# Moving the sample group's state steps beside other projection pairs, and four more gates into pairs, in a one-layer hybrid decoder step

## The chip, the cores and the metric

The kernel runs on one core of one Trainium2 chip, in one launch, and computes one trunk layer in float32. The metric is the time of one execution on the device in microseconds (us). Before the change the median of three runs is 2546.53 us (2541.39 to 2547.61).

## The reference

A prompt group (1024 tokens) and a sample group (8 sequences of one token) go through the same layer. One combined projection `w_in` feeds a gated short convolution, a Mamba-2 state-space branch (SSD) and a cross-attention; sigmoid gates weigh the three outputs.

```python
sc_b, sc_c, sc_x, z, xbc, dt_raw, q, gates = split(xn @ w_in)           # columns 1024,1024,1024,2048,3072,32,1024,3072
y_a = (sc_b * conv3(sc_c * sc_x)) @ w_sc_out
xs, bm, cm = split(silu(conv4(xbc) + b))                                # 32 heads x 64; 4 groups of B and C rows, state 128
dt = softplus(dt_raw + bias);  a = -exp(a_log)
prompt: chunked scan over 8 chunks of 128 tokens, per group of 8 heads
sample: s = s * exp(dt*a) + (dt*x) outer B;   y = s . C                 # one step on a given state, per sequence and head
y_b = group_rmsnorm((y + d*xs) * silu(z)) @ w_ssm_out
y_c = attention(q, mem_k, mem_v) @ w_attn_o
merged = sigmoid(g_a)*y_a + sigmoid(g_b)*y_b + sigmoid(g_c)*y_c;  x += merged @ w_merge_o;  x += swiglu(rmsnorm(x))
```

The sample group's state is 8 sequences x 32 heads x 64 x 128 floats. It is read from HBM, updated once and written back.

## The kernel before, in words

The 1032 tokens (1024 and 8) lie along the free dimension, the features on 128 partitions. A matmul of full precision is three passes over split operands (a high half, made by a cast on ACT, and a low half, made by a subtraction on DVE). A plain projection of 128 columns is `gemm`: 8 slices of k, three passes, three column pieces of 344, so 72 matmuls. Two such projections can be done together by `strassen` as a **pair**: seven half-size products of 24 matmuls of 258 columns, so 168 matmuls. Names of pairs are letter and column block: X (xBC), Z, G (gates), C and B (short convolution). So G0 does gates 0 and 1.

Inside a pair the products run in this order: A (into the accumulator `pa`), T1 (into `pb`), nT2 (into `pa` again, after ACT has copied A's result out, line 299), B21 (into `pc`), T3 (onto `pa`, after ACT's copy of line 321), B22 (onto `pb`), T4 (onto `pa`, after DVE's line 334 has read what T3 left there). Line 227 casts the high halves of the weight forms A, S, T, D on ACT, line 228 makes their low halves on DVE. In instruction names `X4Ah` is the high half of form A of pair X4, `X4Tl` the low half of form T.

The projections come in stages. First z, B and C rows; then 32 pairs from X17 to G14; then the SSD scan of four groups, whose pieces (`ssd_pieces`, `z_pieces`, `group_norm`) are called between the slices of plain projections ("fillers": 8 of q, 8 of gates 16 to 23, then the 8 of `w_sc_out`) by `tick`, at 6.5 pieces a projection; then attention, the other output projections, the merge and the feed-forward part.

In the stage of pairs, blocks i = 0 to 3 are X(4i), X(4i+2), then `sc_pairs(2i)` (pairs C, C, B with their convolutions), then G(4i), G(4i+2). The sample group's steps of group i (`s_pieces`: 8 states) are put into the queue `pend` ahead of `sc_pairs` and are taken three to a pair, where `strassen` calls `tick`. One state is a tile of 128 x 512 in one of two buffers (`act_tile`, tags "ah" and "al", of each of which one buffer is free in this stage): SP loads it from HBM together with its B and C rows, ACT scales its four quarters (line 811), DVE adds (line 813) and reduces (line 817), SP stores it back. The next state in the same buffer can be loaded when the store has landed.

The order of code gives precedence only. The framework that builds the program orders each engine's instructions itself, from the dependences; an instruction may stand well ahead of its place in the code, and on the chip each engine and each DMA queue (SP's, ACT's) runs its list strictly in order.

Of the kernel before, what the change touches and what calls it, by code (L numbers as in the profile page):

```python
# [41 lines left out]
def tile_kernel(ctx: ExitStack, tc, a, o):  # L42
# [611 lines left out]
    def sc_pairs(ct):  # L654
# [22 lines left out]
        o = []  # L677

# [122 lines left out]
    def s_load(g, b):  # L801
        t = act_tile(("ah", "al")[b % 2], f"st{g}_{b}", F32)
        SY.dma_start(b3(t[:, :512], 4), s_rows(a["state_ssm"], g, b))
        SY.dma_start(b3(t[:, 512:768], 2), bc_d[g, b].unsqueeze(0).to_broadcast([P, 2, P]))
        samp[g, b] = t

    def s_step(g, b):
        t = samp[g, b]
        st, junk = b3(t[:, :512], 4), t[:, 768:896]
        for i in range(4):  # L810
            S.activation(st[:, i], st[:, i], AF.Copy, scale=es[:, g * 4 + i, b : b + 1])  # L811
        for i in range(4):
            V.scalar_tensor_tensor(  # L813
                st[:, i], t[:, 512:640], dts[:, g * 4 + i, b : b + 1], st[:, i], op0=ALU.mult, op1=ALU.add
            )
        for i in range(4):
            V.scalar_tensor_tensor(  # L817
                junk, st[:, i], 1.0, t[:, 640:768], op0=ALU.mult, op1=ALU.mult,
                accum_out=ys[:, g * 4 + i, b : b + 1],
            )  # L820

    def s_store(g, b):
        SY.dma_start(s_rows(o["s_ssm"], g, b), b3(samp.pop((g, b))[:, :512], 4))

    def s_pieces(g):

        out = [lambda: s_load(g, 0)]
        for b in range(0, NS, 2):
            out.append(lambda b=b: (s_step(g, b), s_load(g, b + 1)))
            out.append(lambda b=b: (s_store(g, b), s_step(g, b + 1)))  # L830
            out.append(lambda b=b: (s_store(g, b + 1), s_load(g, b + 2) if b + 2 < NS else None))
        return out

    def ssd_pieces(g, xg, bcg):
# [131 lines left out]
        out = [head]  # L966
# [100 lines left out]
    pend.extend([dt_softplus, dt_sums, dt_rows, dt_sample])  # L1067
# [73 lines left out]
    def mem_rms():  # L1141
# [3 lines left out]
        rsqrt(pm, mrs, mst, D, [P, 2], "m")  # L1145

    def mem_t(m, half):
        if half == 0:
            V.tensor_scalar(mem_sb[m], mem_sb[m], mrs[:, m : m + 1], None, op0=ALU.mult)
# [62 lines left out]
    bc_rows()  # L1212
    for i in range(4):
# [11 lines left out]
    pend.extend([None, lambda: b12s.extend(again(rb))])  # L1225
    z_pair(14)
# [639 lines left out]
```

## Time and profile before

| | |
|---|---|
| three runs | 2541.39, 2547.61, 2546.53 us; median 2546.53 |
| profiled execution | 2541.26 us, of which 2539.5 us between the first and the last instruction (the span) |
| busy | PE 2468.5 us, DVE 1512.5, ACT 1029.7, POOL 130.0 |
| stage of pairs, X17 to G14 | 279.67 to 945 us of the span |
| SSD with its fillers | 945 to 1360 us |
| attention and output projections, merge, feed-forward | 1360 to the end |
| DMA | 394.72 MB, mean 155 GB/s |

PE is TensorE, DVE VectorE, ACT ScalarE, POOL GpSimd; SP issues DMAs. A row of the chain or the timeline begins with its start and its length in us. `out<-in` names what is written and read, `xN` the count. `[1.3 <-DMA st]` is the idle time before the instruction and what ended it. Busy PE is not PE at its peak, since matmuls overlap; idle PE is what the tables of waits list.

### The profile page before, as it was taken

What the parts mean: (1) busy time and instruction counts of PE and PEld (TensorE: products, weight loads), DVE (VectorE), ACT (ScalarE), POOL (GpSimd) and SP (SyncE); (2) the same over time, 40 slices, a digit from 0 to 9 for tenths busy, and PEclk for the clock granted to TensorE, in tenths of its full rate; (3) what the DMA queues carried; (4) which work ended last, traced back from release to release, by engine and by line L of the source; (5) the groups of instructions that cost most, each with busy time, mean ns of one, the idle gap of its engine ahead of it and who ended that gap; (6) DMA issues with size and microseconds to landing.
All of it is one profiled execution on the core that took longest, in us unless ns stands there. A gap on an engine that the chain in (4) does not pass through costs nothing.

```text
span 2539.5 us, 44748 instructions
## 1 busy us (share of the span) xinstructions
PE 2468.5 (97%) x18594; PEld 2400.7 (95%) x18594; DVE 1512.5 (60%) x2570; ACT 1029.7 (41%) x1664; POOL 130.0 (5%) x163
## 2 busy tenths in 40 slices
PE   7999999999999999999999989999999999999998
PEld 5999999999999998999989888999999999999998
DVE  6753588486776845665777672444776444453316
ACT  6554454354444445455544341213443333341202
POOL 0300000000000002121120000000000000000000
PEclk9999999999999999999999999999999999999999
DMA  6244435243342555755778977844442222274211
GB/s 203 88 150 158 126 105 155 96 147 119 111 147 80 174 182 168 234 178 188 260 222 281 305 260 239 301 145 151 143 145 93 84 68 84 75 237 139 75 34 68
DMA packets 351610, 394.72 MB, mean 155 GB/s; under 512 B 15798, under 2 KB 289318, under 8 KB 351399
## 3 DMA queue, kind: packets, MB, share of 16 engines
q1 hardware_dynamic: 332254, 338.90, 42.5%
q10 hardware_dynamic: 19153, 52.96, 5.5%
q8 instruction: 146, 2.39, 0.4%
q14 instruction: 57, 0.47, 0.1%
HBM read 283.57 MB, written 108.45 MB: 154 GB/s over the span
## 4 chain that ended last, share of the span: by engine, by line
PE 79%; DVE 9%; DMA 7%; ACT 2%; issue 2%; SPq 0%; POOL 0%; ACTq 0%; DVEq 0%
PE po L195 11%; PE pd L195 8%; PE pm L1624 4%; PE ps_g L195 3%; PE ps_q L195 3%; PE py L906 1%; PE pss L924 1%; PE po L898 1%; DVE ax L649 1%; PE ps_z L195 1%; DMA st<-bc_d 1%; PE X17m L240 1%; PE u20m L240 1%; PE G14m L240 1%; PE G12m L240 1%
## 5 line engine op out<-in xcount | busy, mean ns | idle before, releaser
L1766 DVE TENSOR_TENSOR x<-pd,x 128x1032 f32<-128x1032 f32 x24 | 29.6, 1231 | 127.9 <-PE pd L195 127.9
L853 ACT ACTIVATE r<-r,acum 128x128 f32<-128x128 f32 x256 | 78.7, 391 | 6.0 <-DMA r<-ac_d 5.4
L1265 DVE TENSOR_TENSOR gt<-po,gt 128x1032 f32<-128x1032 f32 x24 | 29.5, 1231 | 58.1 <-PE po L195 54.6
L811 ACT ACTIVATE st<-st,es 128x128 f32<-128x128 f32 x128 | 42.3, 395 | 50.7 <-DMA st<-in_state_ssm_dram 43.7
L885 POOL TENSOR_TENSOR xdd<-xdt,decst 128x512 f32<-128x512 f32 x32 | 40.7, 1271 | 316.6 <-DVE xdt L881 316.6
L649 DVE SCALAR_TENSOR_TENSOR ax<-u,prm,ax 128x1024 f32<-128x1024 f32 x44 | 56.4, 1282 | 0.0
L813 DVE SCALAR_TENSOR_TENSOR st<-st,dts 128x128 f32<-128x128 f32 x128 | 41.6, 348 | 18.8 <-ACT st L811 9.4
L879 DVE TENSOR_TENSOR r<-r,cbm 128x1024 f32<-128x1024 f32 x32 | 39.1, 1221 | 9.8 <-ACT r L854 8.5
L878 ACT COPY bT<-bp 128x128 f32<-128x128 f32 x32 | 8.4, 264 | 88.6 <-DVE cbm L876 88.5
L906 PE MATMUL py<-r,xdt 128*64 128x128 f32 x512 | 35.8, 283 | 4.9 <-issue 4.9
L915 DVE SCALAR_TENSOR_TENSOR x<-x,dpar,yt 128x128 f32<-128x128 f32 x128 | 36.4, 347 | 4.6 <-ACT yt L913 3.8
L817 DVE SCALAR_TENSOR_TENSOR st<-st 128x128 f32<-128x128 f32 x128 | 36.7, 287 | 0.8
L906 PEld LDWEIGHTS py<-r,xdt 128*64 128x64 f32 x512 | 27.9, 139 | 9.2 <-issue 5.8
L902 DVE TENSOR_TENSOR yt<-po,ea 128x512 f32<-128x512 f32 x28 | 19.4, 691 | 28.0 <-PE po L898 28.0
L924 PE MATMUL pss<-xdd,bT 128*128 128x512 f32 x64 | 33.0, 598 | 1.1 <-ACT bT L878 1.0
L854 ACT ACTIVATE r<-r 128x1024 f32<-128x1024 f32 x32 | 33.8, 1058 | 0.5
L937 POOL TENSOR_TENSOR s<-s,cdec 128x512 f32<-128x512 f32 x28 | 33.0, 1178 | 18.9 <-DVE s L930 17.3
L1553 DVE TENSOR_TENSOR gt<-po,gt 128x1032 f32<-128x1032 f32 x8 | 9.9, 1232 | 39.3 <-PE po L195 39.3
L1631 DVE TENSOR_TENSOR x<-pm,xT 128x516 f32<-128x516 f32 x16 | 11.1, 696 | 36.2 <-PE pm L1624 36.1
L1374 DVE SCALAR_TENSOR_TENSOR kc<-kc,qb 128x256 f32<-128x256 f32 x64 | 23.9, 420 | 13.5 <-DMA qb<-qs_d 9.1
L898 PE MATMUL po<-bc,s 128*128 128x128 f32 x224 | 30.1, 278 | 0.0
L898 PEld LDWEIGHTS po<-bc,s 128*128 128x128 f32 x224 | 28.1, 191 | 0.7
(8997 smaller groups left out, 8863.4 us busy)
## 6 DMA issues: line engine op xcount, KB each, us to landing
gt<-gt_d SPq DMA_DIRECT2D x32, 516.0 KB
r<-ac_d SPq DMA_DIRECT2D x32, 512.0 KB
mg_d<-gt SPq DMA_DIRECT2D x24, 516.0 KB
mg<-mg_d SPq DMA_DIRECT2D x24, 516.0 KB
xs_d<-ax ACTq DMA_DIRECT2D x22, 516.0 KB
hr<-h_d SPq DMA_DIRECT2D x22, 516.0 KB
gt_d<-G ACTq DMA_DIRECT2D x16, 516.0 KB
x<-xs_d SPq DMA_DIRECT2D x16, 516.0 KB
```

The costliest lines, as they stand in the source:

```text
L195: PE.matmul(ps[:, n, :CW], wt[:, ks], x[:, n * CW : (n + 1) * CW], start=(k == 0 and i == 0), stop=(k == nk - 1 and i == 2),)
L240: PE.matmul(ps[:, n, :HC], wt[:, ks], x[:, n * HC : (n + 1) * HC], start=(start and kt == 0 and i == 0), stop=(kt == 3 and i == 2), skip_g ...
L649: V.scalar_tensor_tensor(acc[:, :T], u[:, j : j + T], w[j], acc[:, :T], op0=ALU.mult, op1=ALU.add)
L811: S.activation(st[:, i], st[:, i], AF.Copy, scale=es[:, g * 4 + i, b : b + 1])
L813: V.scalar_tensor_tensor(st[:, i], t[:, 512:640], dts[:, g * 4 + i, b : b + 1], st[:, i], op0=ALU.mult, op1=ALU.add)
L853: S.activation(r[:, j, :], r[:, j, :], AF.Relu, scale=-1.0, bias=acum[:, c, h : h + 1])
L879: V.tensor_tensor(r, r, bc(cbm.unsqueeze(1), [P, HPG, P]), op=ALU.mult)
L885: G.tensor_tensor(b3(xdd, HPG), b3(xdt, HPG), bc(decst[:, c, hs].unsqueeze(2), [P, HPG, 64]), op=ALU.mult)
L898: PE.matmul(po[:, t * P : (t + 1) * P], state["s"][:, t * P : (t + 1) * P], bcg[1][:, cs], start=True, stop=True,)
L906: PE.matmul(py[hp : hp + 64, (h // 2) * P : (h // 2 + 1) * P], xdt[:, h * 64 : (h + 1) * 64], r[:, (h % 2) * 4 + h // 2, :], start=True, s ...
L924: PE.matmul(pss, bT, xdd, start=True, stop=True)
L1624: PE.matmul(ps[:, n, :HC], wt[:, ks], x[:, half * HT + n * HC : half * HT + (n + 1) * HC], start=(k == 0 and i == 0), stop=(k == KD - 1 an ...
```

## The change

Six edits:

1. The order of a block becomes X(4i), G(4i), X(4i+2), G(4i+2), C, C, B.
2. The sample group's steps become a list of 34 slots (`s_slots`): slot n stores the previous tile if n is even, does state n, and after an odd n loads the next tile. A tile holds two states (128 x 1024), the B and C rows of four states come in one load of their own (`sr`). Slots are taken three to each pair G and to Z14, two to each pair B and to G16; none in the code of X and C pairs (and none in G0).
3. Gates 16 to 19 become pairs G16 and G18; the fillers of the SSD are now 12 and 8 (q, gates 20 to 23, `w_sc_out`), and the pace is the count of pieces over 20, which is 7.9.
4. The loads of the first SSD group move from the first filler into G18 (`plain`, after T3), and the first weights of q with them; four empty slots follow the group's head.
5. The step sizes (`dt_softplus` and what follows) come one tick later.
6. The scaling of both halves of the memory (`mem_rms`) comes one tick earlier.

```diff
@@ sc_pairs, before the pair B
+        pend.extend([steps.popleft() for _ in range(2)])
@@
-    def s_load(g, b):
-        t = act_tile(("ah", "al")[b % 2], f"st{g}_{b}", F32)
-        SY.dma_start(b3(t[:, :512], 4), s_rows(a["state_ssm"], g, b))
-        SY.dma_start(b3(t[:, 512:768], 2), bc_d[g, b].unsqueeze(0).to_broadcast([P, 2, P]))
-        samp[g, b] = t
+    def s_load(p):
+        g, b = divmod(2 * p, NS)
+        if p % 2 == 0:
+            samp["r"] = ev_tile(f"sr{p}")
+            rows_ = bc_d[g, b : b + 4].rearrange("b w p -> (b w p)")
+            SY.dma_start(samp["r"][:, :1024], rows_.unsqueeze(0).to_broadcast([P, 1024]))
+        samp[p] = act_tile(("ah", "al")[p % 2], f"st{p}", F32), samp["r"]
+        for i in range(2):
+            SY.dma_start(b3(samp[p][0][:, 512 * i : 512 * i + 512], 4), s_rows(a["state_ssm"], g, b + i))
...
-    def s_pieces(g):
-        out = [lambda: s_load(g, 0)]
-        for b in range(0, NS, 2):
-            out.append(lambda b=b: (s_step(g, b), s_load(g, b + 1)))
-            out.append(lambda b=b: (s_store(g, b), s_step(g, b + 1)))
-            out.append(lambda b=b: (s_store(g, b + 1), s_load(g, b + 2) if b + 2 < NS else None))
-        return out
+    def s_slots():
+        n_all = GROUPS * NS
+        steps.append(lambda: s_load(0))
+        for n in range(n_all + 1):
+            def slot(n=n):
+                if n % 2 == 0 and n > 0:
+                    s_store(n // 2 - 1)
+                if n < n_all:
+                    s_step(n)
+                if n % 2 == 1 and n + 1 < n_all:
+                    s_load((n + 1) // 2)
+            steps.append(slot)
+
+    def with_steps(n, pair):
+        pend.extend([steps.popleft() for _ in range(n)])
+        pair()
@@ ssd_pieces
-        out = [head]
+        out = [head] + ([None] * 4 if g == 0 else [])
@@
-    pend.extend([dt_softplus, dt_sums, dt_rows, dt_sample])
+    pend.extend([None, dt_softplus, dt_sums, dt_rows, dt_sample])
@@ mem_rms (from mem_t)
+        for m in range(2):
+            V.tensor_scalar(mem_sb[m], mem_sb[m], mrs[:, m : m + 1], None, op0=ALU.mult)
@@
     for i in range(4):
         xbc_pair(4 * i, 4 * i + 1)
+        with_steps(3 if i else 0, lambda: gate_pair(4 * i))
         xbc_pair(4 * i + 2, 4 * i + 3)
-        pend.extend(s_pieces(i))
+        with_steps(3, lambda: gate_pair(4 * i + 2))
         sc_pairs(2 * i)
-        gate_pair(4 * i)
-        if i < 3:
-            gate_pair(4 * i + 2)
-    flush()
+    with_steps(3, lambda: z_pair(14))
+    with_steps(2, lambda: gate_pair(16))
...
     def plain():
+        loaded["wq0"] = load_raw(wblock(w_in, C_Q), "wq0")
+        load_group(0)
         for kt in range(4):
             split_to(*xforms["T3"][kt], b12s[kt // 2][:, HS[kt % 2]])
-    gate_pair(14, plain)
+    gate_pair(18, plain)
...
-    for i in range(16, 24):
+    for i in range(20, 24):
         fillers.extend(gate_step(i))
...
-    pace[0] = 6.5
-    while pend:
+    pace[0] = len(pend) / (len(fillers) + KD)
+    while fillers or pend:
```

What the engines' lists become at three places. In the names below `st_6107` is the fifth tile of two states, `st_6265` the sixth, `st_5713` the fourth; line 819 is the new number of line 811 (scaling a quarter), 821 that of 813, 825 that of 817.

ACT, from the high half of X4's form A on, before:

```order
L227 CAST X4Ah<-X4r_5393 128x1024
L766 ACTIVATE G_5189<-G_5189 128x516
L227 CAST X4Sh<-X4sa 128x1024
L764 ACTIVATE G_5188<-G_5188 128x1032
L765 DMA gt_d<-G_5188 128x1032
L767 ACTIVATE G_5189<-G2m_5186 128x516
L227 CAST X4Th<-X4sb 128x1024
L768 DMA gt_d<-G_5189 128x1032
L299 COPY u_5399<-X4m_5397 128x516
```

The same stretch of ACT after the change:

```order
L227 CAST X4Ah<-X4r_5328 128x1024
L227 CAST X4Sh<-X4sa 128x1024
L819 ACTIVATE st_6107<-st_6107,es 128x128 x7
L227 CAST X4Th<-X4sb 128x1024
L819 ACTIVATE st_6107<-st_6107,es 128x128
L299 COPY u_5334<-X4m_5332 128x516
L318 COPY u_5335<-X4m_5333 128x516
L227 CAST X4Dh<-X4r_5330 128x512
L321 COPY u_5334<-X4m_5332 128x516
L819 ACTIVATE st_6265<-st_6265,es 128x128 x7
L227 CAST G4Ah<-G4r_5560 128x1024
```

The lone G casts and activations are gone from here, and two tiles' scalings now stand in the X pair: one ahead of the copy of line 299, one ahead of the next pair's `G4Ah`.

DVE, from the low half of X4's form T to line 334 of the same pair, before:

```order
L228 TENSOR_TENSOR X4Tl<-X4sb,X4Th 128x1024
L228 TENSOR_TENSOR X4Dl<-X4r_5395,X4Dh 128x512
L323 TENSOR_TENSOR u_5399<-X4m_5401,u_5399 128x516
L228 TENSOR_TENSOR X6Al<-X6r_5625,X6Ah 128x1024
L334 TENSOR_TENSOR u_5400<-u_5400,X4m_5397 128x516
```

The same stretch of DVE after the change:

```order
L228 TENSOR_TENSOR X4Tl<-X4sb,X4Th 128x1024
L308 TENSOR_TENSOR G4sa<-G4r_5562 128x512
L825 SCALAR_TENSOR_TENSOR sr_5240,ys<-st_5713,sr_5240 128x128
L309 TENSOR_TENSOR G4sa<-G4sa,G4r_5560 128x512
L821 SCALAR_TENSOR_TENSOR st_5713<-sr_5240,dts,st_5713 128x128 x2
L825 SCALAR_TENSOR_TENSOR sr_5240,ys<-st_5713,sr_5240 128x128 x4
L228 TENSOR_TENSOR X4Dl<-X4r_5330,X4Dh 128x512
L323 TENSOR_TENSOR u_5334<-X4m_5336,u_5334 128x516
L228 TENSOR_TENSOR G4Al<-G4r_5560,G4Ah 128x1024
L334 TENSOR_TENSOR u_5335<-u_5335,X4m_5332 128x516
```

The end of tile `st_5713` has come between; the next pair's `Al` stands ahead of line 334 in both lists, and it now needs an `Ah` that stands behind a tile's scalings on ACT.

PE, after the first loads of history (`ps_h`), where the step sizes begin, before:

```order
L520 MATMUL ps_h_0_667<-ident,hist_0_665 128x16 x8
L555 MATMUL ps_dtT<-ident,dtr 128x32 x8
L556 MATMUL ps_dtT<-ident,dtr 8x32
L195 MATMUL ps_C_754<-xnh_115,wC0h 128x344 x3
L195 MATMUL ps_C_754<-xnl_116,wC0h 128x344 x3
```

The same place on PE after the change:

```order
L520 MATMUL ps_h_0_667<-ident,hist_0_665 128x16 x8
L195 MATMUL ps_C_754<-xnh_115,wC0h 128x344 x3
L195 MATMUL ps_C_754<-xnl_116,wC0h 128x344 x3
L195 MATMUL ps_C_754<-xnh_115,wC0l 128x344 x3
L195 MATMUL ps_C_754<-xnh_117,wC0h 128x344 x3
L195 MATMUL ps_C_754<-xnl_118,wC0h 128x344 x3
L195 MATMUL ps_C_754<-xnh_117,wC0l 128x344 x3
L555 MATMUL ps_dtT<-ident,dtr 128x32 x8
```

The transposes of the step sizes have moved behind 18 matmuls of the projection; `ps_C` lies in the accumulator that `ps_dt` held, which DVE reads in line 541. DVE's list is the same in both kernels at this place, and DVE's and PE's lists around the memory's scaling (edit 6) are the same too.

More of the change, by code (lines that the diff above doesn't have):

```diff
@@ L1284, in tile_kernel @@
     for g in range(GROUPS):
[L1285 to L1295 removed]
+        xg, bcg, hold = groups[g]
         pieces = ssd_pieces(g, xg, bcg)
[L1298 removed]
+        if g > 0:
+            pend.extend([lambda g=g: load_group(g), None])
         pend.extend(pieces[:-3])
```

52 lines of the change are left out of this document (29 added, 23 removed).

## The prediction

> **What bounds the kernel now.** I read the busy times first, then the shares of the chain of waits, then the chain in order of time through the stage of pairs, last the list of PE's waits and the engines' timelines at the places that the change touches.
>
> ```profile
> PE 2468.5 (97%) x18594; PEld 2400.7 (95%) x18594; DVE 1512.5 (60%) x2570; ACT 1029.7 (41%) x1664; POOL 130.0 (5%) x163
> PE 79%; DVE 9%; DMA 7%; ACT 2%; issue 2%; SPq 0%; POOL 0%; ACTq 0%; DVEq 0%
> ...
> 447.75 20.23 PE G0m L240 x168
> 467.99 20.23 PE G2m L240 x168
> 508.45 17.34 PE X6m L240 x144
> 593.52 20.23 PE G4m L240 x168
> 654.22 17.34 PE X10m L240 x144
> 738.76 20.23 PE G8m L240 x168
> 799.46 17.34 PE X14m L240 x144
> 884.21 20.23 PE G12m L240 x168
> ...
> 1643.71 78.18 PE po L195 x494
> ```
>
> PE bounds the kernel: 2468.5 of 2539.5 us, so at most 71 us can be won without taking matmuls away. An undisturbed pair lasts 20.23 us (G0, G2), so each of its seven products 2.89. A matmul of a plain projection lasts 78.18/494 = 0.158 us, so one projection of 72 takes 11.39.
>
> The chain shows where pairs are disturbed. X6 starts at 508.45 (its row is six of its seven products) and would end undisturbed 20.23 us later, at 528.68. Three undisturbed pairs (C, C, B) would take 60.69 from there to G4; G4 starts 64.84 after it. The same sum is 64.31 up to G8 and 64.52 up to G12. So C, C, B lose 4.2, 3.6 and 3.8 us; with a like loss in the first block (its X2 is cut up in the chain) the four lose about 15.9. This is what edits 1 and 2 can win at most. The chain names who is late there:
>
> ```profile
> 418.51 3.59 DMA out_s_ssm_dram<-st
> 422.24 2.79 DMA st<-in_state_ssm_dram
> ...
> 829.46 3.00 DMA out_s_ssm_dram<-st
> 833.51 4.75 DMA st<-in_state_ssm_dram
> ...
> PE C1m L240 <- ACT c L299: 1.7, 1, 1.7
> ...
> PE B0m L240 <- ACT b L299: 1.4, 1, 1.4
> ...
> PE ps_dtT L555 <- DVE dtr L541: 2.2, 1, 2.2
> ...
> PE ps_mt L1154 <- DVE mem L1149: 1.0, 1, 1.0
> ...
> PE py L906 <- issue: 4.9, 1, 4.9
> ```
>
> A tile of the sample group's state must be stored before the next can be loaded into its buffer, and ACT, which runs strictly in order, stands with the scalings of line 811 until the load lands; its copy of line 299 comes behind, and PE waits for that 1.7 and 1.4 us.
>
> **The change part by part.** *Edit 3, gates 16 to 19 as pairs.* Four projections leave the SSD: 4 x 11.39 = 45.6 us. Two pairs come: 2 x 20.23 = 40.46. Gain 5.1 us, all on PE. PE is the path on both sides of it, so it counts in full as long as the SSD keeps PE fed.
>
> *Edit 3, what is left in the SSD.* The SSD now has 20 projections between its pieces and not 24.
>
> ```profile
> 945.00:1051.00 106.00, 101.08 (x710) 93.60 (x709) 60.19 (x101) 52.51 (x113) 19.73 (x20) 0.98 0.59 188
> 1051.00:1155.00 104.00, 103.69 (x727) 96.49 (x726) 63.61 (x106) 53.91 (x107) 18.86 (x18) 0.98 0.60 197
> 1155.00:1257.00 102.00, 101.71 (x720) 94.21 (x719) 69.90 (x107) 66.06 (x115) 20.21 (x15) 1.00 0.67 223
> 1257.00:1360.00 103.00, 102.03 (x732) 94.64 (x731) 72.70 (x118) 45.47 (x97) 17.38 (x15) 1.00 0.74 239
> ...
> 980.76 1.05 PE L898 MATMUL po<-bc,s 128*128 128x128 f32 x8
> 987.69 1.05 PE L898 MATMUL po<-bc,s 128*128 128x128 f32 x8
> ```
>
> The columns of the first four rows are the window, its length, and the busy time of PE, PEld, DVE, ACT and POOL, then the clock, the DMA share and GB/s. The four quarters of the SSD leave PE idle 4.9, 0.3, 0.3 and 1.0 us; DVE is at most 72.70/103 = 71% busy. By the order of PE's list, chunks of the first three groups have 24 to 45 matmuls of projections between them, of the last group 17 to 29; after the change all have 17 to 29, as the last group has now. It pays 1.0 us for that. The two `po` rows are one chunk of 6.93 us with 19 such matmuls (3.0 us) and no idle PE between. So three more groups at the last group's idle time, less what they lose now (0.3 each, and the 4.9 told apart below), make 3 x 0.7 = 2 us. Ends: 0, if the 19-matmul chunk is typical; and, since no row shows a dense group with fresh loads at this pace, up to 8 (four times that). Taken: +2.
>
> *Edit 4, first loads inside the last pair.* PE's 4.9 us "issue" before the first `py` is the one stall at the seam. ACT's rows there:
>
> ```profile
> 958.36 2.74 ACT L853 ACTIVATE r<-r,acum 128x128 f32<-128x128 f32 x9 [3.69 <-DMA r<-ac_d]
> 961.12 1.28 ACT L854 ACT_TABLE_LOAD   x1
> ```
>
> The load of `r` is late. It comes into memory which the last G pair's results hold until their store has landed, so an earlier place in the code does not bring it in sooner. What changes is the cover: `py` stood behind 72 + 17 matmuls of projections, now behind 72 + 22. Five more at 0.158 cover 0.8 us of the stall: −0.8 (ends −4.9, if the loads do come sooner, and 0).
>
> *Edits 5 and 6.* The rows of waits price them at most at 2.2 and 1.0.
>
> ```profile
> 60.59 1.27 DVE L541 TENSOR_SCALAR dtr<-ps_dt,bias 32x1032 f32<-32x1032 f32 x1
> 62.01 1.03 PE L555 MATMUL ps_dtT<-ident,dtr 32*128 32x32 f32 x8 [2.21 <-DVE dtr L541]
> 63.02 1.23 PE L195 MATMUL ps_C<-xnh,wC0h 128*128 128x344 f32 x3
> ```
>
> Moving the transposes of line 555 behind 18 matmuls frees PE of that wait, but `ps_C` lies in the accumulator that line 541 is reading until 61.9. So the first `ps_C` waits where `ps_dtT` did. The memory's scaling keeps its place in DVE's and PE's lists. Both: 0 (ends −3.2 together, 0).
>
> *Edits 1 and 2, the sample steps.* The number of scalings, additions, reductions and bytes is the same; each tile is stored in one trip and loaded in one trip, but there are 16 trips of two states. The two buffers remain. The new order of a block doesn't spread the steps over G and Z alone: in the engines' lists one tile falls into the code of C(2i), one on the seam from C(2i) to C(2i+1), and, of the next block, one inside X between its S and T forms, one on the seam from X to G. At these places ACT's copy of line 299, or the next pair's `Ah`, stands behind seven or eight scalings that wait for a load. Prices:
>
> ```profile
> 393.95 1.05 ACT L227 CAST C1Ah<-C1r 128x1024 fp32r<-128x1024 f32 x1 [1.34 <-PE C0m L240]
> ...
> 398.56 1.28 ACT L811 ACTIVATE st<-st,es 128x128 f32<-128x128 f32 x4 [3.55 <-DMA st<-in_state_ssm_dram]
> ...
> 395.71 1.22 DVE L228 TENSOR_TENSOR C1Al<-C1r,C1Ah 128x1024 fp32r<-128x1024 f32 x1
> 396.85 0.69 DVE L309 TENSOR_TENSOR C1sa<-C1sa,C1r 128x512 f32<-128x512 f32 x1
> 397.45 0.69 DVE L334 TENSOR_TENSOR su<-su,C0m 128x516 f32<-128x516 f32 x1
> 399.48 1.14 DVE L813 SCALAR_TENSOR_TENSOR st<-st,dts 128x128 f32<-128x128 f32 x4 [1.34 <-DMA st<-bc_d]
> 400.54 0.28 DVE L817 SCALAR_TENSOR_TENSOR st<-st 128x128 f32<-128x128 f32 x1
> ```
>
> A scaling is 0.3 us, an addition or a reduction 0.28, `Ah` 1.0, `Al` 1.1 (the steps between starts), lines 308, 309 and 334 0.6 each, a copy 0.5. For the trip I take store 3.6 (418.51 gives 3.59) and load 3.0 (between 2.79 and 4.75, nearer the first, which ran with no other tile's load beside it): 6.6 us.
>
> Block 1, counted from X4's first matmul. (c) The pair ahead ends T3 at −5.8; line 334 and five steps of the sample tile follow on DVE, so its store goes out at −3.8, lands at −0.2, the next load lands at 2.9. Seven scalings 5.0, `X4Th` 5.9, one more scaling, the copy of line 299 done at 6.8. PE wants nT2's accumulator at 5.78: a stall of 1.0. (d) `X4Tl` is ready at 7.1; sums of forms and the seven sample steps between them bring the next store to 10.3, the load to 17.1. Seven scalings 19.2, `G4Ah` 20.2, `G4Al` 21.3 on DVE, line 334 behind it 21.9. T4 of X4 needs that line at 17.34 + 1.0: a stall of 3.5. (b) In C(2i), by the same additions, the store goes out at 7.6, the load lands at 14.4, five scalings, `C1Ah`, `C1Al` and line 334 make 18.6 against 17.34: 1.2. A block loses 5.7; three whole ones and (b) of the last, which has no X behind it, 3 x 5.7 + 1.2 = 18.3, against the 15.9 lost now: **+2.4**. Each us on the trip counts ten times (three stalls in three blocks, and one). With the shortest store and load shown, 3.0 and 2.8, the block loses 0.4 + 0.2 + 2.7 and the sum is −5.6; with a trip of 7.4, +10.4; with the longest of both, 3.9 and 4.75, the trip is 8.65 and the sum +23. The 3.9 is SP's, from issuing a store to issuing the load that waits for it:
>
> ```profile
> 854.70 0.38 SPq L823 DMA_DIRECT2D out_s_ssm_dram<-st  x1
> ...
> 858.63 0.37 SPq L803 DMA_DIRECT2D st<-in_state_ssm_dram  x1
> ```
>
> Queues: SP issues each of these loads and stores, and weights wait behind a store that waits for DVE; weight loads stand well over a pair ahead, which covers that. If that cover were gone, a late weight would cost what the store is late, 1 to 3 us. ACT's list has three table loads more than before (46 against 43), 3.8 us at the 1.28 of the row at 961.12; ACT is 41% busy, and they hide in the time in which it waits for PE: 0, at most 3.8.
>
> **Sum**: −5.1 + 2.0 − 0.8 + 0 + 2.4 = −1.5 us on the profiled execution's 2541.26 (1.8 of it outside the span), so 2539.8. The median of the runs stands 5.3 above that execution; I forecast 2545 against 2546.53. Less than 0.3% (7.6 us) of this kernel can't be told from no change.
>
> **Rivals.** *R1, the trip is short: faster.* If two states at a time make store plus load 5.8 us (3.00 + 2.79), (b) and (c) are nearly gone, and the sum is −5.1 + 2 − 0.8 − 5.6 = −9.5: 2537. For it: both ends are rows of the trace. Against it: they never stand in one trip there, and two states are 512 KB.
>
> The Trainium skill ("DMA: Bandwidth & Descriptors", section "Anatomy of one DMA — SWDGE (gpsimd) path") puts a DMA at about 2.0 us and its bytes over 436 GB/s, a fit for another queue than SP's. By it 256 KB take an estimated 2.6 us each way, the trip 5.2, and the sum would be −14.7, thus 2532; the store of 3.59 us and the loads of 2.79 and 4.75 all exceed it, so I give it little of R1's chance.
>
> *R2, the trip is long: slower.* The load at 833.51 took 4.75 us when another tile's stood beside it, and now two loads always go out together, with the B and C rows ahead in the same queue at every second tile. From a trip of 7.5 us on (0.9 more than taken), the stalls (b), (c), (d) make the kernel slower by over 7.6 us; at 8.65 by 19: 2565. Against it: the trip of 418.51 to 425.0 had 6.5.
>
> *R3, the SSD runs dry.* Four projections were its cover. If its engines' own work (DVE 71%) with the waits between them sets the pace, each us that PE lacks is lost. It decides from 11 us on (−3.5 without the SSD's term, and 11, is 7.5: 2554); all of the 45.6 lost give 2589. Against it: the last group already runs at the new density and loses 1.0.
>
> *R4, the steps do less harm in their places than now, with the trip as I took it*, for instance because the loads land ahead of the place where ACT comes to them: with no stall left the sample term is −15.9 and the sum −19.8: 2527. Against it: the lists put them ahead of `Ah` and line 299.
>
> **How the numbers follow.** My sum 0.50 (its own range 2538 to 2552: the trip between 6.0 and 7.3); R1 with R4 0.24; R2 0.18; R3 0.08. Faster: 0.24 and 0.04 of the first, 0.28; slower 0.18 + 0.08 = 0.26; the rest, 0.46, no change. The range leaves out the far end of R2 and R3 (0.10) and of R4 (0.08): 2531 to 2564.
>
> **What the changed profile would show.** G16 and G18 at 20.23 each, and the SSD shorter by 43 to 46 us (415 now). PE idle in its four groups about 1 us each behind the first `py`, whose stall is near 4.1. PE's waits: `ps_C` 2.2 us in place of `ps_dtT`. In blocks 1 to 3: X(4i) waiting about 1 us for ACT's line 299 and 3.5 for DVE's line 334 ahead of T4, C(2i) about 1.2 for line 334; in the chain the store and load of `st` ahead of them, 6.6 us together.
>
> **What would make it wrong**: a trip off by 0.8 us either way, counted ten times; loads of the first `r` that do come before G18's stores; and SSD chunks in which PE waits for DVE or a DMA at 17 matmuls apart.

## The result, and the profile after

| | before | after |
|---|---|---|
| runs beside each other | 2544.28 us median (2541.39 to 2547.61, 4 runs) | 2519.80 us median (2517.93 to 2522.74, 4 runs) |
| profiled execution | 2541.26 us, span 2539.5 | 2517.93 us, span 2516.0 |

The ratio is 0.9904, 95% interval 0.9886 to 0.9922: faster by 24.5 us. The prediction said 2545 with a range from 2531 to 2564, so the time lies 11 us under its lower end. The changed kernel was timed once more later (run e15): 2523.70 us median.

Where the 23.5 us of the span went is read from three stretches, each from the first matmul of its first projection to the first of the next: the pairs (from X17 to the first q), the SSD with its fillers (from there to `wo12`, the third projection of `w_ssm_out`'s first half), and attention (from there to the merge, `pm`). The view by windows of the kernel before, then of the changed one; the columns are the window, its length, the busy time of PE, PEld, DVE, ACT and POOL with counts, the granted clock, the DMA share and GB/s:

```profile
279.50:945.60 666.10, 652.55 (x5386) 649.15 (x5385) 478.25 (x940) 307.84 (x452) 28.83 (x82) 1.00 0.42 128
945.60:1386.70 441.10, 433.17 (x3039) 403.12 (x3039) 284.87 (x446) 229.61 (x446) 76.18 (x68) 0.99 0.67 218
1386.70:1721.70 335.00, 322.77 (x2081) 304.73 (x2080) 173.73 (x346) 95.36 (x181) 0.00 (x0) 0.98 0.75 247
```

```profile
280.30:972.10 691.80, 690.29 (x5722) 688.97 (x5720) 497.31 (x962) 330.54 (x472) 31.31 (x82) 1.00 0.42 129
972.10:1371.20 399.10, 388.63 (x2754) 358.18 (x2754) 275.68 (x442) 216.81 (x434) 82.82 (x68) 0.99 0.71 232
1371.20:1699.50 328.30, 319.06 (x2079) 300.96 (x2078) 172.91 (x344) 94.00 (x180) 0.00 (x0) 0.99 0.75 251
```

| stretch | change in us | of which work moved | left | predicted for what is left |
|---|---|---|---|---|
| start, to X17 | +0.8 | | +0.8 | 0 |
| pairs | +25.7 | +40.5 (G16, G18) | −14.8 | +2.4 |
| SSD and fillers | −42.0 | −45.6 (four projections) | +3.6 | +1.2 |
| attention | −6.7 | | −6.7 | 0 |
| merge to the end | −1.3 | | −1.3 | 0 |

In the table, G16 and G18 are taken at 40.5 us and the four projections at 45.6, the prediction's prices. So two terms made the miss: the sample steps, by 17 us, and attention, which the sum did not contain at all. The stage of pairs is now nearly without idle time: 691.80 less 690.29 is 1.5 us, where it was 13.5. The chain of the changed kernel, in order of time, shows pair behind pair at 20.23 us, also through C, C and B; the one place where the steps still stand in it is X8 (each pair of rows is a store and the load behind it):

```profile
423.81 20.23 PE C0m L240 x168
444.05 20.23 PE C1m L240 x168
464.28 20.23 PE B0m L240 x168
484.51 20.23 PE X4m L240 x168
...
619.44 4.00 DMA out_s_ssm_dram<-st
623.52 4.30 DMA st<-in_state_ssm_dram
...
634.33 2.18 DMA out_s_ssm_dram<-st
636.58 2.82 DMA st<-in_state_ssm_dram
...
644.52 3.17 PE X8m L240 x24
```

PE's waits of the changed kernel (in all, times, longest) have one row of the predicted kind, 0.8 us. The longer rows behind the start of the kernel lie elsewhere: `psp` in attention, the first `py`, line 1304 (the former 1265) near the SSD's end, and `ps_C` of edit 5:

```profile
PE psp L1508 <- ACT pr L1415: 4.7, 3, 2.6
PE py L931 <- issue: 4.2, 1, 4.2
PE po L195 <- DVE gt L1304: 3.9, 1, 3.9
...
PE ps_C L195 <- DVE dtr L541: 2.1, 1, 2.1
...
PE X8m L240 <- DVE u L334: 0.8, 1, 0.8
```

The chain that was predicted for X4 can be laid beside its rows. PE's first matmul of X4 runs at 484.35; the times below that are counted from a pair's start are counted from there. SP's rows, then ACT's, then DVE's of the changed kernel:

```profile
474.75 1.87 SPq L833 DMA_DIRECT2D out_s_ssm_dram<-st  x2
...
480.27 0.93 SPq L811 DMA_DIRECT2D st<-in_state_ssm_dram  x2
...
490.88 0.39 SPq L833 DMA_DIRECT2D out_s_ssm_dram<-st  x1
493.15 0.94 SPq L811 DMA_DIRECT2D st<-in_state_ssm_dram  x2
```

```profile
484.55 2.17 ACT L819 ACTIVATE st<-st,es 128x128 f32<-128x128 f32 x7 [2.05 <-DMA st<-in_state_ssm_dram]
486.62 1.04 ACT L227 CAST X4Th<-X4sb 128x1024 fp32r<-128x1024 f32 x1
...
487.86 0.56 ACT L299 COPY u<-X4m 128x516 f32<-128x516 f32 x1
...
496.19 2.16 ACT L819 ACTIVATE st<-st,es 128x128 f32<-128x128 f32 x7 [2.10 <-DMA st<-in_state_ssm_dram]
498.25 1.03 ACT L227 CAST G4Ah<-G4r 128x1024 fp32r<-128x1024 f32 x1
```

```profile
475.88 0.34 DVE L821 SCALAR_TENSOR_TENSOR st<-sr,dts,st 128x128 f32<-128x128 f32 x1
...
479.86 0.28 DVE L825 SCALAR_TENSOR_TENSOR sr<-st,sr 128x128 f32<-128x128 f32 x1
...
490.25 0.61 DVE L821 SCALAR_TENSOR_TENSOR st<-sr,dts,st 128x128 f32<-128x128 f32 x2
...
500.46 0.69 DVE L334 TENSOR_TENSOR u<-u,X4m 128x516 f32<-128x516 f32 x1
```

The last addition of the tile ends at 476.2 and the store of its last half goes out at once; its last reduction begins at 479.86, 3.6 us later, beside the store's trip. The load goes out at 480.27, lands by 484.5, and ACT's order is as predicted: seven scalings, `X4Th`, a scaling, the copy of line 299, done at 488.4, 4.1 after X4's start. Predicted was 6.8; PE wants it at 5.78. For the second tile the store of its last half goes out at 490.88, right behind the additions, lands in 2.27 and the load in 3.0 (493.15 to 496.19); line 334 ends at 501.1, 16.8 after the start, where PE wants it at 17.34. Predicted was 21.9. In C0, the place (b), line 334 ends 16.4 after the first matmul (439.33 and 0.68, less 423.65); predicted was 18.6.

### The profile page after: what moved, and what is told of

It is laid out like the page before. It is cut to its first block, busy times and chain, and to the rows that moved or that the text cites. A ratio compares the mean times of both kernels' runs of the same rounds, so it can differ in the third digit from the quotient of the medians.

```text
span 2516.0 us, 44833 instructions
## 1 busy us (share of the span) xinstructions
PE 2457.5 (98%) x18642; PEld 2391.0 (95%) x18642; DVE 1521.8 (60%) x2588; ACT 1040.5 (41%) x1679; POOL 139.1 (6%) x163
## 4 chain that ended last, share of the span: by engine, by line
PE 86%; DVE 6%; DMA 5%; ACT 2%; issue 1%; SPq 0%; DVEq 0%; ACTq 0%; POOL 0%
PE po L195 11%; PE pd L195 9%; PE ps_q L195 4%; PE pm L1653 4%; DMA kc<-in_cache_mem_k_dram 1%; PE py L931 1%; PE ps_g L195 1%; PE pss L949 1%; PE po L923 1%; PE ps_z L195 1%; PE X17m L240 1%; PE C3m L240 1%; PE G18m L240 1%; PE Z14m L240 1%; PE C6m L240 1%
## 5 line engine op out<-in xcount | busy, mean ns | idle before, releaser
L821 DVE SCALAR_TENSOR_TENSOR st<-sr,dts,st 128x128 f32<-128x128 f32 x128 | 40.1, 345 | 0.4
L825 DVE SCALAR_TENSOR_TENSOR sr<-st,sr 128x128 f32<-128x128 f32 x128 | 35.3, 286 | 1.1
```

Of the source, the lines that this page charges most:

```text
L821: V.scalar_tensor_tensor(st[:, i], rb, dts[:, g * 4 + i, b : b + 1], st[:, i], op0=ALU.mult, op1=ALU.add)
```

## The experiments

In the table "pairs" is the stretch of pairs, less 40.5 us where the kernel has G16 and G18; the three stretches are of one profiled execution of each kernel. The kernels that have the changed kernel's stage of pairs, or nearly (e6 to e8, e10, e12 to e15), take 651.0 to 652.9 us there, so this stretch tells kernels apart to about 2 us; medians of the same kernel lie 4 us apart (2519.80 and 2523.70).

| run | median us | ratio to before | pairs | SSD | attention |
|---|---|---|---|---|---|
| before | 2543.97 to 2546.65 | | 666.1 | 441.1 | 335.0 |
| changed kernel | 2519.80 | 0.9904 [0.9886, 0.9922] | 651.3 | 399.1 | 328.3 |
| e1 | 2535.18 | 0.9958 [0.9944, 0.9972] | 656.3 | 443.4 | 335.4 |
| e2 | 2537.33 | 0.9971 [0.9961, 0.9981] | 669.4 | 400.8 | 331.3 |
| e3 | 2525.49 | 0.9925 [0.9908, 0.9942] | 655.4 | 399.9 | 327.4 |
| e4 | 2531.34 | 0.9946 [0.9931, 0.9961] | 660.4 | 401.6 | 330.7 |
| e5 | 2526.49 | 0.9923 [0.9904, 0.9942] | 653.6 | 440.3 | 336.0 |
| e6 | 2519.83 | 0.9899 [0.9882, 0.9915] | 651.6 | 399.5 | 327.6 |
| e7 | 2528.11 | 0.9934 [0.9916, 0.9951] | 651.5 | 398.9 | 336.4 |
| e8 | 2532.23 | 0.9948 [0.9931, 0.9964] | 651.0 | 397.1 | 343.3 |
| e9 | 2536.03 | 0.9962 [0.9947, 0.9977] | 664.1 | 440.7 | 332.8 |
| e10 | 2527.48 | 0.9926 [0.9911, 0.9941] | 652.9 | 398.9 | 333.4 |
| e11 | 2539.54 | 0.9978 [0.9968, 0.9988] | 667.7 | 400.8 | 330.2 |
| e12 | 2531.48 | 0.9940 [0.9921, 0.9959] | 652.7 | 398.8 | 337.5 |
| e13 | 2523.42 | 0.9907 [0.9885, 0.9930] | 651.2 | 401.0 | 330.7 |
| e14 | 2519.84 | 0.9896 [0.9875, 0.9916] | 651.6 | 401.1 | 328.4 |
| e15 | 2523.70 | 0.9912 [0.9891, 0.9933] | 651.7 | 399.8 | 327.4 |

### Which edits carry the stage of pairs: e1, e2, e5

e1 puts edits 1 and 2 into the kernel before.

```diff
         xbc_pair(4 * i, 4 * i + 1)
+        with_steps(3 if i else 0, lambda: gate_pair(4 * i))
-        xbc_pair(4 * i + 2, 4 * i + 3)
+        with_steps(0 if i < 3 else 3, lambda: xbc_pair(4 * i + 2, 4 * i + 3))
...
+    pend.extend([steps.popleft() for _ in range(5)])
     z_pair(14)
```

> The kernel before with edits 1 and 2 alone (order of a block and sample steps in slots; the last block has G14 after Z14 as before, so three of its slots go to X14 and five to Z14). Theory: the 14.0 us that the stage of pairs gained come from these two edits and need no other: 2544.3 - 14 = 2530, with C, C, B at 60.7 to 61 us in every block. Rival: the stage gained because the new pairs and the early loads changed what stands behind it: within 5 us of before, 2539 to 2549.

In e1 and in e9 below a few of a group's states are taken ahead of the X pair that gives part of their inputs, and use what stood there before; instructions, tiles and transfers are of the kind and number described. Measured: 2535.18, between the theory and its rival, and a stage 9.8 us shorter instead of 14. Most of the gain needs no other edit. Part of the rest stands in PE's waits at X14 and X12 (1.4 and 1.1 us) and at C7 and C6 (1.1 and 0.9).

e2 is the changed kernel with the old order, the old tiles and the old pieces.

```diff
-        with_steps(3 if i else 0, lambda: gate_pair(4 * i))
         xbc_pair(4 * i + 2, 4 * i + 3)
-        with_steps(3, lambda: gate_pair(4 * i + 2))
+        pend.extend(s_pieces(i))
         sc_pairs(2 * i)
+        gate_pair(4 * i)
+        gate_pair(4 * i + 2)
```

> The changed kernel with edits 1 and 2 undone (old order of a block, one state a tile, old pieces), edits 3 to 6 kept. Theory: what is left of the ledger, 5.1 us for the pairs, less 3.7 that the SSD lost beside fewer projections; the 6 us that attention seems to have gained are a matter of when PE's clock was cut and do not belong to an edit: 2544.3 - 1.4 to - 8 = 2536 to 2543, C, C, B 4 us too long in each block again. Rival: edits 3 to 6 carry the larger part: 2530 or less.

2537.33, as the theory had it. Its stage of pairs is even 3.3 us longer than in the kernel before. Its attention is 3.7 us shorter, though, which the theory did not give to any edit.

e5 takes the steps out of the kernel before and leaves all else in place.

```diff
-        out = [lambda: s_load(g, 0)]
-        for b in range(0, NS, 2):
-            out.append(lambda b=b: (s_step(g, b), s_load(g, b + 1)))
...
+        out = [None] * 13
```

> The kernel before without the sample group's state steps: no loads, scalings, additions, reductions and stores of states (their sums are set to zero and the new states are not written); all pairs and convolutions stay in their places. Theory: the steps alone cost the 15.9 us that C, C, B lost: 2544 - 16 = 2528, C, C, B 60.7 us. Rival: the convolutions' own work on DVE and ACT makes most of that loss: 2538 or more.

2526.49, and the stage 653.6: 12.5 us shorter without the steps. The changed kernel, with all of them, has 651.3. So the steps made that loss, and the changed kernel, with 1.5 us of idle time in the stage, has next to nothing of it left.

### Places or tiles: e3, e4, e9

e3 takes the old order and leaves the slots at G, B and Z14; G0 now has three as well, Z14 two and G16 none.

```diff
         xbc_pair(4 * i, 4 * i + 1)
-        with_steps(3 if i else 0, lambda: gate_pair(4 * i))
         xbc_pair(4 * i + 2, 4 * i + 3)
-        with_steps(3, lambda: gate_pair(4 * i + 2))
         sc_pairs(2 * i)
+        with_steps(3, lambda: gate_pair(4 * i))
+        with_steps(3, lambda: gate_pair(4 * i + 2))
```

> The changed kernel with the old order of a block (X, X, C, C, B, G, G); slots of two states a tile stay three to a G, two to a B, two to Z14. Theory: what cost the time before was that steps stood in C, C and B, whose convolutions fill DVE; the slots in G are what matters, so at most 4 us over the changed kernel, 2520 to 2524. Rival: the alternation of X and G is what gives DVE the room: 8 us or more over it, 2528 or more.

2525.49, a little above the theory's 2524 and below the rival's 2528; the stage is 4.1 us longer than with the new order. PE's waits name the place, ACT's copy of line 321 in the G behind B:

```profile
PE G4m L240 <- ACT G L321: 1.3, 1, 1.3
PE G0m L240 <- ACT G L321: 1.1, 1, 1.1
```

e4 keeps places and order and goes back to one state a tile.

```diff
-                if n % 2 == 0 and n > 0:
-                    s_store(n // 2 - 1)
+                if n > 0:
+                    s_store(*divmod(n - 1, NS))
...
-                if n % 2 == 1 and n + 1 < n_all:
-                    s_load((n + 1) // 2)
+                if n + 1 < n_all:
+                    s_load(*divmod(n + 1, NS))
```

> The changed kernel with one state a tile: each slot stores the state before, does its own and loads the next one (32 trips instead of 16), in the same places and order. Theory that the places decide: at most 4 us over the changed kernel, 2520 to 2524. Rival, two states a tile decide because a trip of store and load (5.3 to 8.1 us in the changed kernel's trace) then stands before every state: 8 us or more over it.

2531.34: the rival. The stage is 9.1 us longer, and PE waits at C again, for line 299 as in the kernel before, and for line 334:

```profile
PE C1m L240 <- ACT c L299: 1.9, 1, 1.9
PE C7m L240 <- ACT c L299: 1.5, 1, 1.5
PE C6m L240 <- DVE su L334: 1.3, 1, 1.3
```

Of the 14.8 us, then, 9.1 need the tile of two states, and 4.1 the order of the block, each taken back alone; that the two add up is not shown. The theory that the places alone decide has fallen.

e9 is e1 with the three slots of X14 given to G0, so that every step from G0 on stands three slots earlier.

```diff
-        with_steps(3 if i else 0, lambda: gate_pair(4 * i))
-        with_steps(0 if i < 3 else 3, lambda: xbc_pair(4 * i + 2, 4 * i + 3))
+        with_steps(3, lambda: gate_pair(4 * i))
+        xbc_pair(4 * i + 2, 4 * i + 3)
```

> Edits 1 and 2 alone once more, with the three slots that stood in X14 given to G0 instead. Theory: the slots in X14 cost the 5 us by which the earlier kernel of this kind fell short in the stage of pairs (idle PE 5.7 us there against 1.5 in the changed kernel); without them the stage is 14 us shorter than before, 2545 - 14 = 2531 or a little less, and attention stays at 335 us as in the kernel before. Rival: the shortfall came with G14 behind Z14: no better than 2535.

2536.03, and the stage only 2.0 us shorter than before. With the same tiles, moved by three slots, PE waits in C for ACT's line 321, behind scalings again:

```profile
PE C4m L240 <- ACT c L321: 3.4, 1, 3.4
...
PE C0m L240 <- ACT c L321: 2.2, 1, 2.2
```

The expectation was wrong. Which slot meets which product is worth 7.8 us here (664.1 against 656.3), nearly as much as the tiles.

### The step that failed: e6, e11

e6 makes each store wait for the last reduction, as the prediction had it.

```diff
+            first = SY.dma_start(late_d[n : n + 1], r[0:1, 256 * (n % 4) : 256 * (n % 4) + P])
+            with tc.issue_after(first.ins):
                 SY.dma_start(s_rows(o["s_ssm"], g, b + i), b3(t[:, 512 * i : 512 * i + 512], 4))
```

> The changed kernel with one step put as the prediction had it: a state's store goes out only after its last reduction (a 512-byte transfer of the last reduction's output into a scratch row stands ahead of each store on SP). Theory: the step that failed is that stores wait for additions alone and go out up to 4 us before the last reduction. With the trips as measured (8.1, 5.3 and 5.1 us) a block then loses 2.4 at line 299 in X, 2.6 and 0.75 at line 334: 18 in all, less the 0.8 lost now: 2520 + 17 = 2537. Rival: the stalls fail to appear for another reason (ACT or DVE does the steps elsewhere): within 4 us of the changed kernel.

2519.83, no difference: my theory of the single wrong step fell. SP's rows at the same place show why:

```profile
477.56 0.38 SPq L837 DMA_DIRECT2D out_s_ssm_dram<-st  x1
...
480.98 0.24 SPq L835 DMA_DIRECT2D late_d<-sr  x1
481.26 0.38 SPq L837 DMA_DIRECT2D out_s_ssm_dram<-st  x1
483.83 0.93 SPq L812 DMA_DIRECT2D st<-in_state_ssm_dram  x2
```

The last half's store does go out five microseconds later (481.26 against 476.2), 3.6 us ahead of X4's start at 484.86, which is close to the predicted 3.8. But it then takes 2.57 us until the load goes out, and the load lands in 3.0, a trip of 5.6 where the changed kernel has 8.3 here. The framework has also set ACT's list anew: `X4Th` stands ahead of the scalings, and of the next tile's scalings two, not seven, stand ahead of `G4Ah`. So the late start cost nothing with the trip and the list that came with it; what it would cost with the predicted ones was not tested.

e11 lengthens the trip: every state is loaded twice.

```diff
+            for _ in range(2):
-            SY.dma_start(b3(samp[p][0][:, 512 * i : 512 * i + 512], 4), s_rows(a["state_ssm"], g, b + i))
+                SY.dma_start(b3(samp[p][0][:, 512 * i : 512 * i + 512], 4), s_rows(a["state_ssm"], g, b + i))
```

> The changed kernel with every state loaded twice in a row into the same place, so that a trip is longer by one load of about 3 us. Theory that the predicted chain (trip, scalings, Ah, Al, line 334) is right in kind and only its trip and its starts were mis-sized: the slack measured in the changed kernel (1.9 us ahead of line 299 in X, 1.1 and -0.8 to 0.6 ahead of line 334) is used up, a block loses about 1.1 + 4.4 + 1.9 us, 22 to 24 in all: 2540 to 2544. Rival: the list is arranged around it and the scalings have other room: within 6 us of the changed kernel.

2539.54, within half a microsecond of the expected band and far from the rival's. The stage is 16.4 us longer, and the gain there is gone. But the sum came out for other reasons than the expected ones. PE's waits stand mostly at the place (b) of the prediction, line 334 in C, and none stands at (d), which was to lose most:

```profile
PE C2m L240 <- DVE su L334: 3.2, 1, 3.2
PE C0m L240 <- DVE su L334: 3.2, 1, 3.2
...
PE C4m L240 <- DVE su L334: 2.3, 1, 2.3
...
PE X8m L240 <- ACT u L299: 1.5, 1, 1.5
```

In X the predicted stall (c) is there: ACT's scalings begin 3.3 us after X4's start (493.40 less 490.06; 0.2 in the changed kernel), and PE waits 0.4, 1.5 and 0.7 us for line 299 in X4, X8 and X12, where the prediction had 1.0 for a load that lands at 2.9. In C it is not the state's trip alone that is late. The chain of e11 through C0, then the changed kernel's row of DVE that uses the weights of C1 first:

```profile
424.87 8.83 DMA C1r<-in_w_in_dram
...
436.13 0.38 SPq L812
...
436.56 3.10 DMA st<-in_state_ssm_dram
...
444.33 0.70 DVE su L334
```

```profile
427.32 0.69 DVE L308 TENSOR_TENSOR C1sa<-C1r 128x512 f32<-128x512 f32 x1 [1.03 <-DMA C1r<-in_w_in_dram]
```

Beside the doubled loads the weights `C1r` take 8.83 us; in the changed kernel they go out at 422.68 and have landed at 427.32, in 4.6. In e11 DVE waits 4.9 us for them (4.3, 3.9 and 3.1 in C3, C5 and C7), the tile's last reductions stand behind that, and the next load goes out behind the reductions, at 436.13. So e11 shows that a late load of a state brings back the stalls of the predicted chain. It does not price the trip, since the weights came late as well.

### The seam and attention: e7, e8, e10, e12, e13, e15

```diff
e7:  -    pace[0] = len(pend) / (len(fillers) + KD)
     +    pace[0] = len(pend) / (len(fillers) + KD - 1)
e12: e7 and
     -    while fillers or pend:
     +    while fillers or pend or len(outs) > 2 * KD + 2:
e10: -        load_group(0)                                (in plain, with wq0's load)
     -        out = [head] + ([None] * 4 if g == 0 else [])
     +        out = [head]
     +    pace[0] = 7.9
e13: -    pend.extend([None, dt_softplus, dt_sums, dt_rows, dt_sample])
     +    pend.extend([dt_softplus, dt_sums, dt_rows, dt_sample])
     (and the memory's scaling back in mem_t)
e8:  e13 and e10, with the pace by its formula (156 pieces over 20)
e15: no change
```

> The changed kernel with the SSD's pieces taken faster: their count over 19 instead of 20, 8.3 instead of 7.9 to a projection, so that the last pieces are done one projection earlier. Theory: PE's wait of 3.9 us for line 1304 near the SSD's end is DVE late with the last group's pieces; it shrinks to 1 us or less, and the half clock after it (3.4 us and more) goes too: 2520 - 4 = 2516. Rival: DVE is late by the splitting of the next inputs, whatever the pace; or the denser chunks lose as much: within 2 us.

> The changed kernel with edits 4, 5 and 6 undone. Theory: they are worth 0 to 1.5 us: the wait before the first py is 4.9 again instead of 4.2, ps_dtT waits 2.2 where ps_C did: 2520 to 2521.5. Rival: one of them carries 3 us or more of the gain: 2523 or more.

> The changed kernel with edit 4 alone undone and the pace kept at 7.9, so that the SSD ends after the same projection. Theory: the 12 us that undoing edits 4 to 6 cost came from the pace: with 156 pieces at 7.8 a rounding left one piece over, attention began one projection later, and PE waited 9.8 us there; edit 4 itself is worth 0.7 us of the first py: 2519.8 + 0.7, at most 2523. Rival: the early loads themselves keep the SSD and the attention on time: 2530 or more.

> The changed kernel with the faster pace of the earlier experiment (8.3), but attention beginning after the same projection as in the changed kernel (all of w_sc_out first). Theory: what the faster pace lost there was the seam (attention one projection early, 336 us instead of 328); with the seam kept, the wait of 3.9 us for line 1304 and the half clock behind it are gone: 2514 to 2518. Rival: the denser pieces themselves lose it: 2525 or more.

> The changed kernel with edits 5 and 6 alone undone. Theory: ps_dtT waits for line 541 again where ps_C did, nothing else moves: 2519.8 within 2 us. Rival: the 2.3 us that the start of the kernel lost when edits 4 to 6 were undone together (idle PE 25.3 us against 23.3 before the pairs, and another spell of half clock) are theirs: 2522 to 2524.

> The changed kernel itself, once more. Theory: its attention takes 328 us again (idle PE 9.2, one spell of half clock), so that the 7 us are the order of PE's list there: 2518 to 2522, attention within 2 us. Rival: the 7 us are spread between executions: attention at 331 us or more.

e7 gave 2528.11 and e12 2531.48: a faster pace does shrink the wait for line 1304 from 3.9 to 1.2 us, and loses more in attention, in e12 as in e7. The theory fell twice. e8 lost 9 to 12 us (against 2523.70 and 2519.80): the rival. The largest piece is one wait of 9.8 us at attention's end, ahead of the first projection of `w_attn_o` (1621.6); attention had begun one projection later. e10 avoids that and still loses 4 to 8 us, not 0.7. e13 has 2523.42, which was the rival's band; but e15, the changed kernel itself, has 2523.70, so edits 5 and 6 are worth nothing that shows, as predicted. e15's median lies above the expected band too, but its attention is at 327.4 again, so the 7 us there come back with the kernel.

Where attention loses its time can be read from the traces. Its length, less PE's idle time in it and less half of the time that PE's clock was granted at half, is 316 to 318 us in all 17 profiles. The kernel before has 12.2 us idle and 10.2 at half clock there, the changed one 9.2 and 3.4: 3.0 and 3.4 us of the 6.7.

What goes with the difference is PE's list in attention, which no edit names. Between the scores of a block of queries and the transposes of its probabilities the list has, for the four blocks of the second head, 11, 23, 22 and 21 projection matmuls in nine kernels (the changed one, e2, e3, e4, e6, e11, e13, e14, e15), and their attention takes 327.4 to 331.3 us. It has 13, 26, 25 and 30 or 37 in seven (before, e1, e5, e7, e9, e10, e12): 332.8 to 337.5. e8, with a third list, takes 343.3. The framework sets this order. The faster list comes with edits 3 and 4 and their pace: e1, with neither edit, has the old first three counts, and so have e10, without edit 4, and e7 and e12, with a faster pace. The list was not changed by itself, so that it is the cause is argued and not shown; why fewer matmuls between should be faster was not settled.

### The clock: e14

```diff
             state["bT"] = S.copy(bT, bp[:, :P]).ins
+            if g == 0 and c == 0:
+                spare = sm_ps("spare")
+                for i in range(27):
+                    PE.transpose(spare[:, (i % 4) * P : (i % 4) * P + P], bT, ident)
```

> The changed kernel with 27 transposes of no use (into a spare accumulator) ahead of the first py, where PE waits 4.2 us. Theory that a wait of PE over some 2 us is followed by 3.4 us or more at half clock, and that this costs time by itself: the wait before py shrinks to 0.5 us or less, the granted clock stays at 1.0 there, and the kernel gains 1.7 us though py begins no sooner: 2518. Rival: the half clock in the records is a consequence without a price of its own, or follows the matmuls that come after: 2520 or slower, by what the transposes delay.

2519.84. The granted clock behind the first `py`, and in the second row behind the wait for line 1304, by windows of the changed kernel; then its row of the first `py` on PE's timeline:

```profile
991.00:994.40 3.40, 3.40 (x23) 3.07 (x24) 0.49 (x2) 3.25 (x8) 0.19 (x1) 0.53 0.31 113
1342.30:1349.10 6.80, 5.09 (x17) 4.73 (x18) 6.22 (x6) 0.04 (x1) 0.00 (x0) 0.50 1.03 359
```

```profile
990.97 1.97 PE L931 MATMUL py<-r,xdt 128*64 128x128 f32 x16 [4.22 <-issue]
```

The same two views of e14:

```profile
991.50:994.90 3.40, 3.40 (x32) 3.21 (x33) 0.29 (x1) 2.97 (x7) 0.19 (x1) 1.00 0.37 96
```

```profile
991.45 1.09 PE L935 MATMUL py<-r,xdt 128*64 128x128 f32 x16 [2.70 <-DVE r L908]
```

The clock stayed whole: 16 matmuls take 1.09 us instead of 1.97. But the transposes did not fill the wait. PE is idle for 2.7 us ahead of `py` and for 1.2 ahead of the transposes, 3.9 in all against 4.2. What made room for them is work: in the changed kernel 72 and 19 projection matmuls stand ahead of the first `py`, in e14 the 72 alone, and 19 at 0.158 are 3.0 us that now come behind it. The SSD is no shorter (401.1 against 399.1 and 399.8). So the 1.7 us that the theory expected from the clock were outweighed, and e14 does not decide what half clock costs.

## Why the prediction was wrong, point by point

**The pairs, −5.1:** right. G16 and G18 take 20.23 and 20.24 us in the chain, and from G0 on all pairs but X8 run undisturbed.

**The sample steps, +2.4: the step that failed.** Measured −14.8. The form of the chain was right: ACT's order, `Ah`, `Al`, line 334 are in the trace as written, X8's 0.8 us is stall (d), and e11 has stall (c). Two of its terms were mis-sized. The first is the start: "line 334 and five steps of the sample tile follow on DVE, so its store goes out at −3.8" tied the store to the tile's last steps, which are reductions. A store needs the additions alone, and went out at −8.1 in X4. The second is the trip, taken as "6.6 us": where the last half goes out alone it is 5.0 (634.33) and 5.3 (490.88). The long trip of X, 8.3 at 619.44, errs the other way, but starts so much earlier that its load lands by 0.2 instead of 2.9. For X4's second tile the store went out at 6.5 instead of 10.3: 2.5 us of that because `X4Tl` was ready at 4.6 instead of 7.1, as the first tile was early, and 1.2 because four reductions were not waited for. How the 17 us divide between start and trip stays open: e6 took back the first start alone and lost nothing, but with another trip and another list. The kernel before had said so: in its chain two additions stand right ahead of the store that the prediction quoted (418.51), and no reduction.

```profile
417.96 0.53 DVE st L813 x2
```

Each us on the trip was to count ten times; no run measures that, since e11 delayed the weights too.

R1 had the right sign and named the trip; its 5.8 gave 2537, still too slow, for it kept the late starts. The sentence on the Trainium skill ("DMA: Bandwidth & Descriptors", section "Anatomy of one DMA — SWDGE (gpsimd) path"), 2.6 us each way, gave a trip of 5.2 and 2532. Two of this case's trips agree with its sum (2.18 and 2.82, 2.27 and 3.0) better than with the 6.6 that I took; the trip of X, 4.00 and 4.30, does not. I was wrong to give it little. R4, that no stall is left, was the outcome in the stage: its −15.9 stands against −14.8. The 15.9 was a little high itself: without the steps the old order is 12.5 us shorter (e5).

**The SSD, +2.0 and −0.8:** the sum is +3.6. The first `py` waits 4.2 instead of 4.9, near the predicted 4.1; this is partly luck, for 72 and 19 matmuls stand ahead of it, not 72 and 22, and two more than before cover 0.3 us and not 0.8. Edit 4 is worth more than that in all: without it (e10) the kernel is 4 to 8 us slower, most of it in attention. What was not foreseen is the wait of 3.9 us for line 1304 at the seam, with 6.8 us at half clock. R3 did not happen: the first three groups run at the new density without a loss that the waits list.

**Edits 5 and 6, 0:** right. `ps_C` waits 2.1 us where `ps_dtT` did.

**Attention, not in the sum, −6.7:** the missing term. I compared the engines' lists around the edits and not behind them; the list in attention was there to be compared, and differs. Its price, less idle time and less half clock, could not have been read from the trace of before.

**Chances:** no case of the prediction had the stage without stalls together with a gain elsewhere; R1 with R4 had 0.24, and only R4's 2527 came near.

## What to carry to other kernels

Before pricing a wait for a transfer, ask which instruction last writes what it reads, and of a tile stored in parts count the trip from its last part. A chain with slack has a threshold: price the slack first, then the slope; here a shift by three slots turned 9.8 us of gain in the stage into 2.0. An experiment that makes one transfer longer can delay its neighbours: look at their rows before the result is read as the price of the first. And where a framework arranges the lists, compare them behind the edit too, as far as they differ: 7 us came from a stage that no line of the diff touches.

## What the runs showed of the hardware

A wait of PE is followed by half clock more often the longer it is. Over the profiles of the kernel before, the changed one and e1 to e15, between 64 and 2480 us of each span, take the gaps in PE's busy time that stand alone (less than 0.25 us of others from 4 us ahead to 4 us behind) and count those at which, or within 3.5 us behind which, a spell of half clock begins: of 130 gaps from 0.7 to 1.5 us, none; of 30 from 1.5 to 2.5, 8; of 12 from 2.5 to 3.5, 8; of 31 longer ones, 31. A spell lasts 3.4 us or a multiple of it. The Trainium skill ("TensorE: Matmul & The Clock Gate", section "Part 1: The HAM clock gate (the "warmup" mystery)") has the clock halved after an idle window of about 3.4 us and windows that run freely. The length of the spells agrees with it. That the whole window must be idle does not: 16 of the 42 gaps from 1.5 to 3.5 us were followed by half clock, and so were all 30 from 3.5 to 6.8 us, in which a window that runs freely would lie whole only by chance.

The last half of a tile's store, 256 KB, landed in 2.2 to 2.3 us (634.33, 490.88) when its first half had long gone out, and in 4.0 (619.44) where both went out within 2 us, with weight loads issued at 617.49 and 621.39 beside them. A weight load took 8.83 us beside doubled loads of states (e11, 424.87) and 4.6 without.
